# Four weight buffers and seven sets of activations at other places within a 512-byte line, in a two-block transformer kernel on one core

## The chip, the cores and the metric

The kernel runs on one core of one Trainium2 chip. Its time is the device time of one execution, in microseconds (us); with one core, that core is also the slowest. The profile is of one execution, and its span is the time from the first to the last of the program's own instructions.

## What is computed

Two blocks run one after the other on x of 256 tokens by 1024 columns, all in fp32. Cut to the matrix work, which is nearly all of the time:

```python
def first_block(...):
    h = rmsnorm(x, norm_mix_g[l])
    proj = h @ w_in[l]                      # 1024 x 8192: conv, stick-breaking, retention, gates
    up = jnp.einsum('bsnw,nwd->bsnd', branches, w_branch[l])
    x = x + jnp.sum(gates * up, axis=2) @ w_o[l]
    x = x + memory_attention(rmsnorm(x, norm_xa_g[l]), mem_n, w_xq[l], w_xkv[l], w_xo[l])
    x = x + squared_relu_mlp(rmsnorm(x, norm_mlp_g[l]), w_up[l], w_down[l])   # 1024 x 4096 and back
    return rmsnorm(x, final_g)

def second_block(...):
    # layer 0 mixes with ssd_mixer, layer 1 with mla_attention; after each mixer:
    h = layer_norm(DN_ALPHA * h + mix, ln_mix_g[i], ln_mix_b[i])
    ff = conv_ffn(h, ffn_up[i], ffn_conv_w[i], ffn_conv_b[i], ffn_down[i])    # 1024 x 5632, 2816 x 1024
    h = layer_norm(DN_ALPHA * h + ff, ln_ffn_g[i], ln_ffn_b[i])
```

## The kernel before

**Split products.** Every large product is taken three times in the type fp32r: each fp32 operand is split into a high part h and a rest l, and `mm3` adds h·h, h·l and l·h in PSUM. So each block of a weight matrix is needed as `wh` and `wl`, and each activation as `ah` and `al` (or another pair of that kind: `br`, `mt`, `memT`, `oT`, `gT`, `yT`, `cT`, each with an h and an l).

**Weights.** `chunk_plan` cuts all weights into some 200 chunks of at most 2048 columns of fp32 for each of the 128 partitions, and the host lays them out in the order of use. For each chunk `pump` issues one DMA from SyncE into `wr` (two buffers), `copy` makes `wh` from it on ScalarE, `sub` makes `wl` on VectorE. `wh` and `wl` have four buffers each, taken in turn by `ring`, so that the splits of later chunks run while TensorE works on an earlier one.

**Two kinds of products.** In `wstat` the weights are the stationary operand and the activations move: for each of eight blocks k of 128 rows, 256 columns of `ah` or `al` pass a 128x128 block of `wh` or `wl`. The rows of a profile write this as `mm<-ah,wh` (moving operand first). The order inside one k is (ah, wh), (al, wh), (ah, wl). In `xstat` the activations are stationary and up to 512 columns of the weights move: `mm<-wh,ah`, `mm<-wl,ah`, `mm<-wh,al`, and `mm<-wh,gTh` and so on in the down projections. Each matmul has a weight load (LDWEIGHTS, engine PEld) of its own, which runs beside the matmul before it.

**Order.** The program is recorded with an order of its own: `tick` decides from a table of estimated durations (class `Plan`) which waiting task or split is recorded next. Addresses do not enter into it. All recorded instructions stand at one line of the code (L284, the wrapper that records), so rows are told apart by their tiles.

**Places.** `new_act` gives each of seven layers its `ah` and `al`, from a pool with one buffer each, so all seven stand at one address. The `wh` and `wl` pools follow each other in SBUF, and a buffer is 8192 bytes long, a multiple of 512. Modulo 512, the built program has all four buffers of `wh` and all four of `wl` at 288, and `ah` and `al` at 480 in every layer. `br`, `gT`, `yT` and the `oT` of the first block are at 288, `mt`, `memT` and `cT` at 480. A row of `ah` for one k is 1024 bytes, a block of stationary columns 512 bytes, and all strides inside the buffers keep the place modulo 512, but for a few blocks of 320 and 384 columns in the attention's first product. `gap` puts an unused tile into a pool, to move what follows; only the attention of the second block does so.

Of the kernel before, what the change touches and what calls it, by code (L numbers as in the profile page):

```python
# [7 lines left out]
F32R = mybir.dt.float32r  # L8
# [8 lines left out]
P = 128  # L17
D = 1024
S = 256
ALPHA = 4 ** 0.25  # L20
NG = 8
RAW, HELD = 2, 4
# [64 lines left out]
def chunk_plan():  # L87
# [62 lines left out]
    def ffn(layer):  # L150
        for j in range(22):
            add("fu", K8, (f"fup{layer}", 128 * j, 128), (f"fup{layer}", 2816 + 128 * j, 128))
        xwide("fd", f"fdn{layer}", 22)

    ffn(0)
    for k in range(0, 8, 2):
        add("kvq", range(k, k + 2), ("kvd", 0, 320), ("qd", 0, 384))
# [305 lines left out]
        self.sync = Lane(plan, nc.sync, "sp")  # L463


class Kern:
    def __init__(self, nc, tc, a, dbg=None):
        self.at = Plan()
        self.nc, self.tc, self.a, self.dbg = Engines(nc, self.at), tc, a, dbg
        self.plan, _ = chunk_plan()  # L470
        self.nch = len(self.plan)
        self.n_dma = self.n_prep = self.n_half = self.n_get = self.n_done = 0
        self.raw, self.held, self.subs = {}, {}, []
        self.bg = []
        self.floor = 0.0
        self.turns = {}
        self.blocked, self.table = False, None
        self.work = self.skew = 0.0
        self.sums = np.concatenate([[0.0], np.cumsum([len(ks) * max(n, P) * UNIT for _, ks, _, n, _ in self.plan])])

# [12 lines left out]
            self.n_dma += 1  # L493

    def ring(self, pool, tag, dtype, n):
        t = pool.tile([P, 2048], dtype, tag=tag, name=tag)
        rows = self.turns.setdefault(tag, [])
        self.at.reuse(t, rows[-n] if len(rows) >= n else None)
        rows.append(t)
        return t  # L500
# [316 lines left out]

    def new_act(self):

        return (self.acts.tile([P, 8, S], F32R, tag="ah", name="ah"), self.acts.tile([P, 8, S], F32R, tag="al", name="al"), [0, 0])  # L820

    def ready(self, act, k, *taus):
        if len(act) == 3:
# [433 lines left out]
    def memory(self, x, mt, memT, mt_close):  # L1257
        nc, a = self.nc, self.a
        act = self.new_act()
        ga = self.bcast("xa", self.gb, "gb")  # L1260
        mp, mp_close = self.open("mem")
        oT = self.pair(mp, "oT", 8)

        kT = (mp.tile([P, 8, S], F32R, tag="kT", name="kT"), mt[1])
# [152 lines left out]
    def ssd(self, h, act):  # L1417
        nc, a = self.nc, self.a
        pool, close = self.open("ssd")
        yT = self.pair(pool, "yT", 16)  # L1420
        decs = Slots(self, pool, "dec", [P, 4, 384], F32, 4)
        r512 = Slots(self, pool, "r512", [P, 2, S], F32, 7)
        for i in range(2):
            t = self.gb.tile([P, D], F32, tag="gb", name="gb")
# [266 lines left out]
    def ffn(self, layer, h, act):  # L1691
        nc = self.nc
        pool, close = self.open(f"ffn{layer}")
        gT = self.pair(pool, "gT", 22)
        r512 = Slots(self, pool, "r512", [P, 2, S], F32, 6)

        def col(t):
            c = COLS["fcw"] + 132 * layer + t
            b = COLS["fcb"] + 44 * layer + t
            return lambda j: self.pcol[:, c + 44 * j:c + 44 * j + 1], self.pcol[:, b:b + 1]  # L1700

        def up_out(j):
            def run(pt, t):
                acc = yield from r512.wait()
                gs = [self.taps(acc[:, i, :], pt[:, 256 * i:256 * i + 256], 3, *col(j + 22 * i)) for i in range(2)]
                for g in gs:
                    next(g)
                yield "dve"
                for _ in zip(*gs):
                    pass  # L1710
                self.free(pt)
                yield "act"
                nc.scalar.activation(acc[:, 0, :], acc[:, 0, :], AF.Silu)
                yield "dve"
                nc.vector.tensor_mul(acc[:, 0, :], acc[:, 0, :], acc[:, 1, :])
                yield "act"
                yield from self.split((gT[0][:, j, :], gT[1][:, j, :]), acc[:, 0, :])
                r512.put(acc)
            return run

        tasks = []
        self.wmixed("fu", act, 8, [up_out(j) for j in range(MIXED["fu"][layer])], tasks)
        self.dump(("h1", "h2")[layer], h)
        for j in range(MIXED["fu"][layer], 22):
            self.wstat("fu", act, 8, up_out(j), tasks)
        g_, b_ = self.bcast(f"lfg{layer}", self.gb, "gb"), self.bcast(f"lfb{layer}", self.gb, "gb")
        act = None if layer else self.new_act()
        ps = self.xstat("fd", [2] * 11, self.lhs(gT), [(0, 512), (512, 1024)], tail=TAIL["fd"][layer],
                        before=lambda c: self.until(*tasks[2 * c:2 * c + 2]),
                        after=lambda t, p, got: self.layernorm(t, h, g_, b_, act, p, got))  # L1730
        close()
        return act
# [235 lines left out]
    def program(self):  # L1968
        nc, tc, a = self.nc, self.tc, self.a
        cs = []  # L1970

        def pool(name, bufs=1, **kw):
            cm = tc.tile_pool(name=name, bufs=bufs, **kw)
            cs.append(cm)
            return cm.__enter__()

        cp = pool("const")
        self.gb = pool("gb", 2)  # L1980
        self.dram = pool("dram", space=bass.MemoryType.DRAM)
        self.acts = pool("acts")
        cq = pool("small")
        self.tiny = pool("tiny", 4)
        self.tk = Slots(self, pool("tk"), "tk", [P, D], F32, 2)
        self.wraw, self.whi, self.wlo = pool("wraw", RAW), pool("whi", HELD), pool("wlo", HELD)
        pp = pool("ps", space=PSUM)
        self.mm = Slots(self, pp, "mm", [P, 512], F32, 4)
        self.sm = Slots(self, pp, "sm", [P, 512], F32, 4)

        x = cp.tile([P, 2, D], F32, tag="x", name="x")
        self.cst = cst = cq.tile([P, NCST], F32, tag="cst", name="cst")
        self.ones = cp.tile([P, P], F32, tag="ones", name="ones")
        nc.vector.memset(self.ones, 1.0)

        row = self.tk.get()
        o, w = ROWS["mix"]
        nc.sync.dma_start(out=row[0:1, :], in_=a["prow"][0:1, o:o + w])
        halves = [slice(512 * n, 512 * n + 512) for n in range(2)]
        for c in halves:  # L2000
            nc.sync.dma_start(out=x[:, 0, c], in_=a["x"][0:P, c])
        nc.sync.dma_start(out=cst[:, 0:P], in_=a["cst"][:, 0:P])
        self.pump(1)
        nc.sync.dma_start(out=x[:, 1, :], in_=a["x"][P:2 * P, :])
        self.pump()
        nc.sync.dma_start(out=cst[:, P:], in_=a["cst"][:, P:])
        gs = [self.mm.get() for c in halves]
        for pt, c in zip(gs, halves):
            self.mm1(pt, self.ones[0:1, :], row[0:1, c], True)
        self.tk.put(row)  # L2010
        self.pcol = cp.tile([P, NCOL], F32, tag="pcol", name="pcol")
        nc.sync.dma_start(out=self.pcol, in_=a["pcol"])
        self.ident, self.nu, self.ut = (cst[:, CST[n]:CST[n] + P] for n in ("ident", "nu", "ut"))
        self.at.one = cq.tile([1, 2], F32, tag="one", name="one")
        nc.vector.memset(self.at.one, 1.0)
        self.neg1 = cp.tile([P, P], F32, tag="neg1", name="neg1")
        nc.vector.memset(self.neg1, -1.0)
        self.mhalf = cq.tile([P, 2], F32, tag="mhalf", name="mhalf")
        nc.vector.memset(self.mhalf, -0.5)
        self.identb = cp.tile([P, P], BF16, tag="identb", name="identb")  # L2020
        nc.vector.tensor_copy(self.identb, self.ident)

        self.maskb = cp.tile([P, P], BF16, tag="maskb", name="maskb")
        nc.vector.memset(self.maskb, 0.0)
        nc.gpsimd.affine_select(out=self.maskb, in_=self.maskb, compare_op=ALU.is_ge, fill=-1e30, base=0,
                                pattern=[[-1, P]], channel_multiplier=1)

        act = self.new_act()
        self.until(self.spawn(self.rms(0, x, Halves(gs), act), first=True))

        def second():
            yield from self.rms(1, x, Halves(gs), act)
            for pt in gs:
                self.mm.put(pt)

        self.spawn(second(), first=True)
        mt, memT, mt_close = self.mixers(act)
        self.spawn(self.angles(cp))
        act, close = self.memory(x, mt, memT, mt_close)
        act = self.mlp(x, act, close)  # L2040
        act = self.ssd(x, act)
        act = self.ffn(0, x, act)
        act = self.attention(x, act)
        self.ffn(1, x, act)
        self.drain()
        assert self.n_get == self.nch
        for cm in reversed(cs):
            cm.__exit__(None, None, None)
# [21 lines left out]
```

## Time and profile before

| what | value |
|---|---|
| median of 2 runs | 1242.21 us (1240.86 to 1243.56) |
| the profiled execution | 1244.83 us |
| its span | 1243.1 us |
| busy PE, PEld, DVE, ACT, POOL | 1224.7, 1120.8, 853.9, 717.0, 53.5 us |
| matmuls and weight loads | 8468 each |
| read from HBM | 225.27 MB, 182 GB/s over the span |

A matmul's duration in the trace runs from its start to its modelled end and overlaps the next one's. How fast matmuls follow each other is read from starts, or from a stretch: in a stretch of length T that is filled with matmuls of one kind, each lasting d, a count of n means one start every (T + d) / n.

### The profile page before, as it was taken

How to read it: one execution, taken by the hardware profiler on the slowest of the kernel's cores; microseconds unless marked ns; L12 is line 12 of the kernel's file. 1: busy time of each engine (PE TensorE's matmuls, PEld its weight loads, DVE VectorE, ACT ScalarE, POOL GpSimd, SP SyncE). 2: the span in 40 equal slices, each digit the busy share in tenths (PEclk: the TensorE clock that was granted, in tenths of full speed). 3: DMA queues.
4: the chain of work that ended last, by engine and by line, in shares of the span. 5: the costliest groups of instructions: out<-in, count | busy, mean ns of one | idle time of the engine just before them, and what ended most of it. 6: DMA issues, size and time to landing. Idle time of an engine off the chain costs nothing.

```text
span 1243.1 us, 20768 instructions
## 1 busy us (share of the span) xinstructions
PE 1224.7 (99%) x8468; PEld 1120.8 (90%) x8468; DVE 853.9 (69%) x1378; ACT 717.0 (58%) x1181; POOL 53.5 (4%) x85
## 2 busy tenths in 40 slices
PE   7999999999999999999999999999999999999997
PEld 5978999989989998889999898999988888999986
DVE  5666847666746665446787797877765866888853
ACT  5666546446536554335788765666644575666641
POOL 0011000000000000000111201000000000000000
PEclk9999999999999999999999999999999999999999
DMA  7643355546544546524656555555573443455560
GB/s 254 235 167 127 146 196 219 179 156 228 176 152 159 214 172 221 201 106 166 227 190 233 193 174 194 187 172 202 184 259 118 161 181 123 172 197 182 213 256 35
DMA packets 35425, 227.71 MB, mean 183 GB/s; under 512 B 4321, under 2 KB 4993, under 8 KB 11522
## 3 DMA queue, kind: packets, MB, share of 16 engines
q1 hardware_dynamic: 35330, 226.39, 50.8%
q8 instruction: 66, 1.08, 0.4%
q14 instruction: 29, 0.24, 0.1%
HBM read 225.27 MB, written 1.10 MB: 182 GB/s over the span
## 4 chain that ended last, share of the span: by engine, by line
PE 95%; DVE 3%; DMA 1%; issue 0%; ACT 0%; POOL 0%; SPq 0%; POOLq 0%; DVEq 0%; ACTq 0%
PE mm L284 85%; PE sm L284 9%; DVE wl L284 1%; DVE x L284 1%; DMA wr<-wts 0%; DVE tk L284 0%; DMA cst<-cst 0%; POOL rs L284 0%; ACT wh L284 0%; DVE ln L284 0%; DVE al L284 0%; SPq L284 0%; POOLq L2066 0%; ACT r L284 0%; ACT ah L284 0%
## 5 line engine op out<-in xcount | busy, mean ns | idle before, releaser
L284 DVE TENSOR_TENSOR wl<-wr,wh 128x1024 fp32r<-128x1024 f32 (+3 forms) x408 | 479.4, 1198 | 173.7 <-ACT wh L284 173.0
L284 ACT CAST wh<-wr 128x1024 fp32r<-128x1024 f32 (+3 forms) x408 | 403.6, 1029 | 162.4 <-PE mm L284 87.9
L284 PE MATMUL mm<-ah,wh 128*128 128x256 f32 (+1 forms) x1496 | 421.1, 281 | 0.0
L284 PE MATMUL mm<-ah,wl 128*128 128x256 f32 (+1 forms) x1496 | 417.5, 279 | 0.0
L284 PE MATMUL mm<-al,wh 128*128 128x256 f32 (+1 forms) x1496 | 417.4, 279 | 0.0
L284 PEld LDWEIGHTS mm<-ah,wh 128*128 128x128 f32 (+1 forms) x1496 | 283.0, 189 | 1.6 <-issue 1.1
L284 PEld LDWEIGHTS mm<-ah,wl 128*128 128x128 f32 (+1 forms) x1496 | 281.0, 188 | 0.1
L284 PEld LDWEIGHTS mm<-al,wh 128*128 128x128 f32 (+1 forms) x1496 | 280.5, 188 | 0.4
L284 DVE SCALAR_TENSOR_TENSOR r<-mm,pcol,r 128x255 f32<-128x255 f32 (+2 forms) x212 | 86.9, 474 | 38.6 <-ACT r L284 38.6
L284 PE MATMUL mm<-wl,ah 128*128 128x512 f32 (+3 forms) x320 | 106.3, 338 | 3.1 <-DVE wl L284 3.0
L284 PE MATMUL mm<-wh,ah 128*128 128x512 f32 (+3 forms) x320 | 108.6, 345 | 0.0
L284 PE MATMUL mm<-wh,al 128*128 128x512 f32 (+3 forms) x320 | 105.9, 337 | 0.5 <-DVE al L284 0.5
L284 PE MATMUL mm<-wh,gTh 128*128 128x512 f32 x304 | 96.3, 391 | 0.0
L284 PE MATMUL mm<-wh,gTl 128*128 128x512 f32 x304 | 95.6, 389 | 0.0
L284 PE MATMUL mm<-wl,gTh 128*128 128x512 f32 x304 | 95.6, 390 | 0.0
L284 ACT ACTIVATE r<-mm,pcol 128x256 f32<-128x256 f32 x96 | 48.9, 560 | 46.9 <-PE mm L284 46.9
L284 PEld LDWEIGHTS mm<-wl,ah 128*128 128x128 f32 x320 | 60.3, 189 | 10.2 <-DVE wl L284 4.9
L284 PEld LDWEIGHTS mm<-wh,gTl 128*128 128x128 f32 x304 | 57.1, 188 | 11.8
L284 PEld LDWEIGHTS mm<-wl,gTh 128*128 128x128 f32 x304 | 57.1, 188 | 11.8
L284 PEld LDWEIGHTS mm<-wh,gTh 128*128 128x128 f32 x304 | 56.7, 188 | 12.0 <-issue 0.6
L284 PEld LDWEIGHTS mm<-wh,al 128*128 128x128 f32 x320 | 60.3, 189 | 7.0 <-DVE al L284 1.1
L284 PEld LDWEIGHTS mm<-wh,ah 128*128 128x128 f32 x320 | 60.3, 189 | 6.6 <-issue 0.7
(296 smaller groups left out, 1581.8 us busy)
## 6 DMA issues: line engine op xcount, KB each, us to landing
wr<-wts SPq DMA_DIRECT2D x186, 1024.0 KB, 4.9
wr<-wts SPq DMA_DIRECT2D x11, 768.0 KB, 4.3
gb<-prow SPq DMA_DIRECT2D x12, 512.0 KB, 6.8
dec<-rows SPq DMA_DIRECT2D x8, 768.0 KB, 7.5
wr<-wts SPq DMA_DIRECT2D x4, 704.0 KB, 4.2
wr<-wts SPq DMA_DIRECT2D x4, 512.0 KB, 7.0
tk<-mem SPq DMA_DIRECT2D x2, 512.0 KB, 7.9
out<-x SPq DMA_DIRECT2D x4, 256.0 KB, 2.1
```

What stands on the lines that cost most here:

```text
L284: r = f(*args, **kw)
```

## The change

Six edits, none of which adds, removes or reorders an instruction: on each of the five engines the instructions stand in the same order before and after, with the same tiles and shapes. One wait is added: of the second group of `dec` (the decay tiles of the state-space mixer), the first AFFINE_SELECT on GpSimd waits for ScalarE too, beside its DMA.

- The buffers of `wh` and `wl` become 16 elements (64 bytes) longer, so that the four of a ring stand 64 bytes apart modulo 512.
- `ah` and `al` get 128 elements more, and each layer takes its part from a start of its own, out of `PLACES` (bytes).
- Gaps stand ahead of `wl`, behind it, and at the start of the pools of the memory attention, the state-space mixer and the two feed-forward layers.
- The scratch for dynamic DMAs is 1 KB instead of 16 KB a partition; no DMA of this kernel uses it. It makes room for the rest.

```diff
+PLACE = 16
+PLACES = (0, 144, 256, 32, 288, 0, 16)
...
     def ring(self, pool, tag, dtype, n):
-        t = pool.tile([P, 2048], dtype, tag=tag, name=tag)
+        t = pool.tile([P, 2048 + (PLACE if dtype is F32R else 0)], dtype, tag=tag, name=tag)
...
     def new_act(self):
-        return (self.acts.tile([P, 8, S], F32R, tag="ah", name="ah"), self.acts.tile([P, 8, S], F32R, tag="al", name="al"), [0, 0])
+        at = PLACES[self.n_act] // 4
+        self.n_act += 1
+        h, l = (self.acts.tile([P, 8 * S + 128], F32R, tag=n, name=n)[:, at:at + 8 * S].rearrange("p (k s) -> p k s", s=S) for n in ("ah", "al"))
+        return (h, l, [0, 0])
...
         mp, mp_close = self.open("mem")
+        self.gap(mp, 288)
...
         pool, close = self.open("ssd")
+        self.gap(pool, 256)
...
         pool, close = self.open(f"ffn{layer}")
+        self.gap(pool, (32, 256)[layer])
...
-        self.wraw, self.whi, self.wlo = pool("wraw", RAW), pool("whi", HELD), pool("wlo", HELD)
+        self.wraw, self.whi = pool("wraw", RAW), pool("whi", HELD)
+        self.gap(pool("gap0"), 256)
+        self.wlo = pool("wlo", HELD)
+        self.gap(pool("gap1"), 256)
...
-    nc = bacc.Bacc("TRN2", target_bir_lowering=False, num_devices=1)
+    nc = bacc.Bacc("TRN2", target_bir_lowering=False, num_devices=1, dynamic_dma_scratch_size=1024)
```

Places modulo 512 in the two built programs:

| tiles | before | after |
|---|---|---|
| `wh`, `wl`, the four buffers in the order of use | 288, 288, 288, 288 | 288, 480, 416, 352 |
| `wr` (both buffers) | 288 | 288 |
| `ah`, `al`: mixers, memory attention, MLP | 480, 480, 480 | 480, 112, 224 |
| `ah`, `al`: state-space mixer, feed-forward 0 | 480, 480 | 0, 256 |
| `ah`, `al`: latent attention, feed-forward 1 | 480, 480 | 480, 496 |
| `br`; `memT`, `mt`; `cT` | 288; 480; 480 | 288; 480; 480 |
| `oT`, `kT`, `qs`, `vt` of the memory attention | 288 | 64 |
| `gT` of MLP, feed-forward 0, feed-forward 1 | 288, 288, 288 | 288, 320, 32 |
| `yT` | 288 | 32 |

## Rows read from the trace of the kernel before

**Rows 1.** The page: span, then busy time (share) and instructions by engine.

```profile
span 1243.1 us, 20768 instructions
PE 1224.7 (99%) x8468; PEld 1120.8 (90%) x8468; DVE 853.9 (69%) x1378; ACT 717.0 (58%) x1181; POOL 53.5 (4%) x85
...
PEclk9999999999999999999999999999999999999999
```

**Rows 2.** The page, chain that ended last: shares of the span by engine, by line.

```profile
PE 95%; DVE 3%; DMA 1%; issue 0%; ACT 0%; POOL 0%; SPq 0%; POOLq 0%; DVEq 0%; ACTq 0%
```

**Rows 3.** Waits of PE: for whom, us in total, times, longest.

```profile
PE sm L284 <- DVE tk L284: 3.1, 1, 3.1
PE mm L284 <- DVE wl L284: 3.0, 3, 2.0
PE mm L284 <- DMA tk<-prow: 2.4, 1, 2.4
```

**Rows 4.** Stretches: busy us (x instructions) of PE, PEld, DVE, ACT, POOL; clock; DMA share, GB/s.

```profile
139.00:180.00 41.00, 41.00 (x364) 41.00 (x363) 23.24 (x29) 21.53 (x33) 0.00 (x0) 1.00 0.54 193
240.00:252.00 12.00, 12.00 (x102) 12.00 (x101) 11.62 (x22) 5.94 (x9) 0.00 (x0) 1.00 0.68 254
...
402.00:468.00 66.00, 66.00 (x562) 66.00 (x562) 44.06 (x50) 37.58 (x50) 0.00 (x0) 1.00 0.55 200
484.00:540.00 56.00, 56.00 (x249) 46.40 (x248) 24.55 (x21) 20.07 (x20) 0.00 (x0) 1.00 0.52 188
...
798.00:898.00 100.00, 100.00 (x851) 100.00 (x850) 82.19 (x145) 63.22 (x109) 0.00 (x0) 1.00 0.52 179
1083.00:1172.00 89.00, 89.00 (x788) 89.00 (x787) 75.25 (x134) 58.44 (x99) 0.00 (x0) 1.00 0.56 194
```

**Rows 5.** PE's groups by form, feed-forward 0, 798 to 898 us.

```profile
L284 PE MATMUL mm<-ah,wl 128*128 128x256 f32 x284 | 79.9, 281 | 0.0
```

**Rows 6.** The same for feed-forward 1, 1083 to 1172 us.

```profile
L284 PE MATMUL mm<-ah,wl 128*128 128x256 f32 x262 | 72.4, 276 | 0.0
```

**Rows 7.** PE's groups by form over the span: busy us, mean ns of one | idle before.

```profile
L284 PE MATMUL mm<-ah,wh 128*128 128x256 f32 x1488 | 418.9, 281 | 0.0
L284 PE MATMUL mm<-ah,wl 128*128 128x256 f32 x1488 | 415.3, 279 | 0.0
L284 PE MATMUL mm<-al,wh 128*128 128x256 f32 x1488 | 415.2, 279 | 0.0
...
L284 PE MATMUL mm<-wh,gTl 128*128 128x512 f32 x304 | 95.6, 389 | 0.0
...
L284 PE MATMUL mm<-wh,al 128*128 128x512 f32 x144 | 57.3, 398 | 0.5 <-DVE al L284 0.5
...
L284 PE MATMUL mm<-wl,ah 128*128 128x256 f32 x144 | 40.4, 281 | 0.3 <-DVE wl L284 0.3
...
L284 PE MATMUL mm<-brh,wl 128*128 128x256 f32 x96 | 27.2, 283 | 0.0
...
L284 PE MATMUL mm<-memTh,wl 128*128 128x256 f32 x64 | 17.7, 276 | 0.0
```

**Rows 8.** All operations on tile brh: ns min/median/max, first and last start us.

```profile
L284 PEld LDWEIGHTS mm<-brh,wl x96: 187/192/193, 182.6 to 251.6; 128*128 128x128 f32 x96
L284 PE MATMUL mm<-brh,wl x96: 279/283/284, 182.7 to 251.7; 128*128 128x256 f32 x96
```

**Rows 9.** The page, groups of DVE and ACT that make wl and wh.

```profile
L284 DVE TENSOR_TENSOR wl<-wr,wh 128x1024 fp32r<-128x1024 f32 (+3 forms) x408 | 479.4, 1198 | 173.7 <-ACT wh L284 173.0
L284 ACT CAST wh<-wr 128x1024 fp32r<-128x1024 f32 (+3 forms) x408 | 403.6, 1029 | 162.4 <-PE mm L284 87.9
```

**Rows 10.** GpSimd in order of time: start us, us, the second group of dec among them.

```profile
631.01 1.23 POOL L284 TENSOR_SCALAR_AFFINE_SELECT dec<-dec 128x512 f32<-128x512 f32 x2
633.48 3.51 POOL L284 TENSOR_SCALAR_AFFINE_SELECT dec<-dec 128x512 f32<-128x512 f32 x2 [1.24 <-DMA dec<-rows]
```

More of the change, by code (lines that the diff above doesn't have):

```diff
@@ L477, in __init__ @@
         self.blocked, self.table = False, None
+        self.n_act = 0
         self.work = self.skew = 0.0
```

## The prediction

> **What bounds the kernel now.** I read the page first: PE is busy for 1224.7 of 1243.1 us, the clock is granted in full in all 40 slices [rows 1], and 95% of the chain that ended last is PE's [rows 2]. The longest wait of PE in the whole run is 3.1 us [rows 3]. So nothing that makes PE wait is worth a per cent, and the time can only move if matmuls follow each other at another rate. Busy time can't show that, because a matmul's row overlaps the next one's. The count of starts in a filled stretch can.
>
> Four stretches hold nothing but matmuls of 256 moving columns (up to a few small ones at their edges). By (T + d) / n, feed-forward 0 starts one every (100 + 0.281) us / 851 = 117.8 ns, the MLP's up projection one every (66 + 0.281) / 562 = 117.9 ns, feed-forward 1 one every (89 + 0.276) / 788 = 113.3 ns, and the gates one every (41 + 0.276) / 364 = 113.4 ns [rows 4]. The first and the third run the same code with the same shapes from the same places, at the same full clock, with DVE at 82% and 85% and ACT at 63% and 66%. PE's own row tells the two rates apart: a matmul lasts 281 ns at the slower [rows 5] and 276 ns at the faster [rows 6]. The reader is to see a stream with two stable rates, which keeps one of them through a whole stage of twenty chunks.
>
> A third rate is in the branch product, where the moving `br` and all `wh` and `wl` stand at 288: one start every (12 + 0.283) / 102 = 120.4 ns, and 283 ns a matmul [rows 4, 7]. There the weight load takes 192 ns in the median, with 187 ns as the shortest [rows 8]: what is slow is the pair, the load and the matmul beside it. With `memT` at 480 against 288, the distance that `ah` has, a matmul lasts 276 ns [rows 7]. So distance 0 (modulo 512) was slow in all its chunks, and distance 192 is either.
>
> What the neighbours do is not the cause, as far as rows show: DVE and ACT are as busy at the fast rate as at the slow one [rows 4].
>
> With 512 moving columns the load has twice the time. The MLP's down projection, `gT` at 288 against 288, starts one every (56 + 0.389) / 249 = 226.5 ns [rows 4], twice the fast rate, and 389 ns a matmul [rows 7]. With `ah` at 480 as the stationary side, one lasts 398 ns [rows 7]; part of that is waits at the start of a layer.
>
> **What the best rate would return.** Durations of 276, 281 and 283 ns go with 113.3, 117.8 and 120.4 ns from start to start, so 5 ns of duration are about 4.5 ns of time.
> - `ah`, `al` moving, 3 x 1488 matmuls at 279 ns (281 in the first group, which also holds the waits at the start of a chunk): 3 of 5 ns above the fast rate, so 60% of them are slow. 4464 x 0.6 x 4.5 ns = 12.1 us [rows 7].
> - `br`: 3 x 96 x (120.4 - 113.3) ns = 2.0 us [rows 7].
> - Weights moving with 256 columns, 3 x 144 at 281 ns: all slow, 432 x 4.5 ns = 1.9 us [rows 7].
> - Weights moving with 512 columns against `ah`, 3 x 144 at 398 against 389 ns: 9 x 0.9 x 432 = 3.5 us at the most, since waits are in it; I take 2 [rows 7].
> - The other products of 512 columns are at the fast rate: nothing.
>
> Together 18 us, 1.4% of the span. No row of 256 columns goes under 276 ns in its mean, so I have no ground for a rate below 113.3 ns.
>
> **The change part by part.**
>
> *Four places for the weight buffers, seven for the activations.* The distance of moving to stationary side was 192 in every chunk of `ah`. Now it is another one in each of four chunks in turn: 192, 0, 64, 128 in the mixers and the latent attention, for instance, and four others in each other layer. For none but 0 and 192 does a row of 256 moving columns in `wstat` show a rate. The ends: all at 113.3 ns gives the 18 us back. All at 120.4 ns costs 4464 x (0.4 x 7.1 + 0.6 x 2.6) ns = 19.6 us, and 9 x 0.9 x 912 ns = 7.4 us if the 512 columns of `gT` took on the 398 ns: +27 us. Between ends so far apart I go by the row that is nearest to a chunk of its own: today a stage stays at one rate for all its chunks because each meets the last one's distance again. With the distance changed at each chunk, a slow rate is no longer handed on to the next by equal places. I take half of the slow excess of `ah` as gone: 6 us of the 12, and 2 of the 3.9 with weights moving.
>
> *Branch product.* One chunk in four keeps distance 0. The other three get 320, 384 and 448. At the middle rate for these the gain is 216 x 2.6 ns = 0.6 us, at the best one 216 x 7.1 ns = 1.5 us. I take 1.
>
> *The gaps* move `gT`, `yT`, `oT`, `kT` and `vt`. With 512 moving columns, distance 0 runs at the best rate already, so there is little to gain; about 0.5 us lies in the small products. I take 0, with the 7.4 us above as the price if it goes wrong.
>
> *Making the splits.* The casts of 1029 ns and the subtractions of 1198 ns [rows 9] write to other places. Should each become 5% longer, 408 x 60 ns = 24 us more on DVE would bring it from 69% to 71% of the span; PE's stream hides that, since its waits for `wl` are 3.0 us in all [rows 3]. If they became shorter, it would return no more than those 3.0 us. I take 0.
>
> *The added wait* on GpSimd stands ahead of the select at 631 us (1.23 us for two), which feeds decay tiles [rows 10]. Behind it in GpSimd's queue are the next two selects, which started at 633.5 us after a wait of 1.24 us for their own DMA. An early ACT instruction costs nothing; a late one would first use up that 1.24 us, and past it delays the decays of one of four groups, beside chunks of products that PE has in hand. I take 0, and 3 us (the length of the later selects) as its upper end.
>
> *The scratch* is not read or written by any instruction: 0.
>
> Sum: -6 - 2 - 1 = -9 us. Against the profiled execution, 1244.8 us (its span of 1243.1 and 1.7 around it), that is 1235.8 us. This execution lies 2.6 us above the median of the two runs shown, and the three times differ by 4.0 us, about what one stage like feed-forward 0 costs by its choice of rate (851 x 4.5 ns = 3.8 us). I hold the sum against the median, 1242.2: 1233 us.
>
> [...] The rows show one and the same kind of matmul at 276, 281 and 283 ns, at full clock [rows 5 to 7]. [...]
>
> **The rivals.**
> - *The place does not set the rate.* Something else at the start of a stage picks one of the two rates, and it picks as before, or by another throw. For it: feed-forward 0 and 1 differ at the same places [rows 4]. Against it: `br` is slow in all its chunks [rows 8]. The time is 1242 us, give or take the 4 us of one stage's throw.
> - *Every stream at the best rate.* The places are such that load and moving stream do not meet in any layer. For it: 113.3 ns is stable over twenty chunks once reached. Against it: the mixers and the latent attention now have distance 0, the slow one, in a quarter of their chunks. The time is 1242 - 18 = 1224 us.
> - *More meetings than before.* With four distances in each layer, most of them near each other, a load that meets the moving stream costs the 120.4 ns of `br` in most chunks. At three chunks of four the mean is 118.6 ns against 113.3 + 0.6 x 4.5 = 116.0 now: 4464 x 2.6 ns = +11.6 us, 1254 us. It turns from gain to loss when more than 2.7 / 7.1 = 38% of the chunks are at 120.4 and the rest at 113.3. For it: distance 0, which the kernel before had in `br` alone, now comes in the mixers too. Against it: only 0 is seen to be always slow.
>
> **How the numbers follow.** A measurement of this kernel can tell about 2% from no change. The forecast of 1233 us gets 0.45, no effect of the place 0.17, all at the best rate 0.20, more meetings 0.18. The best rate everywhere is 1.4% below the median, so faster by over 2% (below 1217 us) needs a rate that no row shows: 0.02. Slower by over 2% (above 1267 us) needs nearly all of the +27 us: 0.03. The range from 1222 to 1250 us holds the forecast, the best rate and no effect, and part of the losing case. The forecast's own range is 1227 to 1239.
>
> **What would show each step right or wrong.** In the profile after, the group of 256 columns with `ah` over the span should have a mean of 277 to 278 ns in place of 279, `br` 279 to 281 in place of 283, and the stretches of the MLP's up projection and of feed-forward 0 should hold chunks at both 113 and 118 ns, with changes at the borders of chunks. The matmuls of 512 columns with `gT` should stay at 389 ns, PE's waits below 10 us in all. If whole stages still keep one rate, or if feed-forward 1 falls back to 118 ns, the step on the chunks is wrong. A mean of 281 ns or more would make it slower than before.

## The result and the profile after

The changed kernel takes 1259.53 us (median of 1259.25 and 1259.81) against 1242.21: 1.0139 times as long, with an interval of 1.0091 to 1.0188. The profiled execution after is the one of 1259.25 us, with a span of 1257.5; the one before had a span of 1243.1 [rows 1], so 14.4 us are to be found.

The page of the changed kernel: span, busy time by engine, the chain's shares, and the groups that make `wl` and `wh`.

```profile
span 1257.5 us, 20769 instructions
PE 1240.6 (99%) x8468; PEld 1129.6 (90%) x8468; DVE 854.5 (68%) x1378; ACT 716.4 (57%) x1181; POOL 53.4 (4%) x85
...
PE 95%; DVE 2%; DMA 1%; issue 0%; SPq 0%; ACT 0%; POOL 0%; POOLq 0%; DVEq 0%
...
L284 DVE TENSOR_TENSOR wl<-wr,wh 128x1024 fp32r<-128x1024 f32 (+3 forms) x408 | 480.0, 1199 | 178.2 <-ACT wh L284 177.3
L284 ACT CAST wh<-wr 128x1024 fp32r<-128x1024 f32 (+3 forms) x408 | 403.0, 1028 | 163.2 <-PE mm L284 94.6
```

Only PE has changed: 15.9 us more busy time with the same 8468 matmuls, while DVE, ACT and GpSimd stand where they stood [rows 1], and cast and subtraction take what they took [rows 9]. PE's waits have not grown either [rows 3]; these are the changed kernel's (for whom, us in total, times, longest):

```profile
PE mm L284 <- DVE wl L284: 2.7, 3, 1.6
PE mm L284 <- DMA tk<-prow: 2.4, 1, 2.4
PE sm L284 <- DVE tk L284: 2.3, 1, 2.3
```

So the time lies in the rate. The stretches of the changed kernel that answer to [rows 4], with the same columns:

```profile
139.00:180.00 41.00, 41.00 (x354) 41.00 (x353) 22.33 (x28) 20.52 (x33) 0.00 (x0) 1.00 0.53 189
402.00:468.00 66.00, 66.00 (x569) 66.00 (x567) 45.11 (x51) 37.02 (x49) 0.00 (x0) 1.00 0.53 192
484.00:540.00 56.00, 56.00 (x244) 45.56 (x244) 23.61 (x20) 20.15 (x21) 0.00 (x0) 1.00 0.53 190
798.00:898.00 100.00, 100.00 (x850) 100.00 (x849) 81.32 (x146) 63.55 (x111) 0.00 (x0) 1.00 0.52 187
1083.00:1172.00 89.00, 89.00 (x761) 89.00 (x760) 73.86 (x134) 57.91 (x100) 0.00 (x0) 1.00 0.51 178
```

By (T + d) / n, with the durations shown below, the gates went from one start every 113.4 ns to 116.6, the MLP's up projection from 117.9 to 116.5, feed-forward 0 from 117.8 to 118.0, feed-forward 1 from 113.3 to 117.3, and the down projection with `gT` from 226.5 to 231.1. The clock is 1.00 in all of them. What was slow gained little or nothing; what was fast lost.

PE's groups by form over the span, changed kernel, beside [rows 7]:

```profile
L284 PE MATMUL mm<-ah,wh 128*128 128x256 f32 x1488 | 420.5, 283 | 0.0
L284 PE MATMUL mm<-ah,wl 128*128 128x256 f32 x1488 | 417.0, 280 | 0.0
L284 PE MATMUL mm<-al,wh 128*128 128x256 f32 x1488 | 416.7, 280 | 0.0
...
L284 PE MATMUL mm<-wh,gTl 128*128 128x512 f32 x304 | 97.0, 394 | 0.0
...
L284 PE MATMUL mm<-wh,al 128*128 128x512 f32 x144 | 57.4, 399 | 0.5 <-DVE al L284 0.5
L284 PE MATMUL mm<-wl,ah 128*128 128x256 f32 x144 | 40.6, 282 | 0.3 <-DVE wl L284 0.3
...
L284 PE MATMUL mm<-brh,wl 128*128 128x256 f32 x96 | 26.8, 279 | 0.0
```

`ah` and `al` moving are 1 to 2 ns a matmul slower, not 1 to 2 ns faster; `gT` is 5 ns slower; `br` is 4 ns faster. To see what that is in time I added up, over each whole trace, the time from each matmul's start to the next one's, by what the matmul multiplies:

| products (matmuls) | before, us | after, us | difference |
|---|---|---|---|
| `ah`, `al` moving, 256 columns (4488) | 523.8 | 532.6 | +8.8 |
| `gT` and weights, 512 columns (912) | 207.9 | 211.9 | +4.0 |
| weights moving past `ah`, 512 and 256 columns (864) | 159.0 | 160.1 | +1.1 |
| `memT`, `oT`, `yT`, `cT`, `mt` (930) | 181.1 | 183.6 | +2.5 |
| `br` (288) | 34.7 | 33.8 | -0.9 |
| fp32 products and the rest | 126.3 | 125.3 | -1.0 |

Together +14.5 us, against the 14.4 between the two spans.

Then chunk by chunk. The MLP's up projection in the changed kernel, four chunks in a row, PE's groups by form; the moving place stands 256, 320, 384 and 448 bytes (modulo 512) above that of the weights:

```profile
L284 PE MATMUL mm<-ah,wl 128*128 128x256 f32 x15 | 4.2, 283 | 0.0
...
L284 PE MATMUL mm<-ah,wl 128*128 128x256 f32 x15 | 4.1, 276 | 0.0
...
L284 PE MATMUL mm<-ah,wl 128*128 128x256 f32 x15 | 4.2, 281 | 0.0
...
L284 PE MATMUL mm<-ah,wl 128*128 128x256 f32 x15 | 4.1, 276 | 0.0
```

283, 276, 281, 276 ns go with 120.0, 113.4, 118.5 and 113.6 ns from start to start, and this rotation comes back in every group of four. Once it is under way, feed-forward 0 has 118.3, 116.8, 119.8 and 117.4 ns in rotation, at distances 480, 288, 352 and 416; feed-forward 1 has 116.6 to 118.3 at 16, 80, 144 and 208, where it had 113.3 throughout.

### The profile page after: what moved, and what is told of

Its sections match the earlier page's. It is cut to its first block, busy times and chain, and to the rows that moved or that the text cites. A ratio compares the mean times of both kernels' runs of the same rounds, so it can differ in the third digit from the quotient of the medians.

```text
span 1257.5 us, 20769 instructions
## 1 busy us (share of the span) xinstructions
PE 1240.6 (99%) x8468; PEld 1129.6 (90%) x8468; DVE 854.5 (68%) x1378; ACT 716.4 (57%) x1181; POOL 53.4 (4%) x85
## 4 chain that ended last, share of the span: by engine, by line
PE 95%; DVE 2%; DMA 1%; issue 0%; SPq 0%; ACT 0%; POOL 0%; POOLq 0%; DVEq 0%
PE mm L284 86%; PE sm L284 9%; DMA wr<-wts 1%; DVE wl L284 1%; DVE x L284 0%; SPq L284 0%; DVE tk L284 0%; DVE al L284 0%; POOL rs L284 0%; DVE ln L284 0%; ACT wh L284 0%; POOLq L2080 0%; ACT r L284 0%; DVEq L2080 0%; ACT ah L284 0%
```

## The experiments

The theory that this suggests: the distance of the moving place from the stationary one, modulo 256, sets the rate of a chunk by itself, and the chunk before it has no say. Rivals: that the changing of distances from chunk to chunk costs time, whichever they are; that a wait, a gap or the smaller scratch does it; and, from the prediction, that the place does not matter at all.

Edits are against the kernel before. Every kernel has the 1 KB scratch of the first, and in each all places that are not named are those of before. "Filled stretch" is PE alone from 806 to 890 us, inside feed-forward 0: busy us (x matmuls), clock, DMA share, GB/s; the spacing is (84 + d) / n with d of 0.276 to 0.283 us. Each kernel ran beside the kernel before on the same chip; the second time given is that kernel's. The ratio and its 95% interval are worked out from all runs, so the ratio is not always the quotient of the two medians. In all kernels `ring` and `new_act` are those of the change, with `PLACE` and all `PLACES` at 0 unless the edit says otherwise; so `ah` and `al` are 512 bytes longer everywhere, which keeps all places modulo 512.

### The scratch alone

```diff
-    nc = bacc.Bacc("TRN2", target_bir_lowering=False, num_devices=1)
+    nc = bacc.Bacc("TRN2", target_bir_lowering=False, num_devices=1, dynamic_dma_scratch_size=1024)
```

> Control: of the change only the scratch of 1 KB, all operands at their places modulo 512 of before. Theory A (the distance moving minus stationary, modulo 256, sets the rate of a matmul): the time of before, 1242 us, mean of the 256-column group of ah 279 ns, gT at 389 ns. Rival (the scratch or the absolute address costs): up to 17 us more, gT above 392 ns.

1240.28 us against 1240.23: 1.0003 [0.9988, 1.0019]. The scratch costs nothing. The profile taught something else; its filled stretch:

```profile
806.00:890.00 84.00, 84.00 (x744) 1.00 0.53 189
```

84.276 / 744 = 113.3 ns, where the profiled execution of before had feed-forward 0 at 117.8 [rows 4]. No place differs, so at distance 192 a stage has either of two rates. This profile's span is 1237.1 us, 6.0 under that of [rows 1], and 4.8 us of it are in the products of `ah`: feed-forward 0 and the first four chunks of moving `ah` (27 to 49 us) ran at 117.8 ns in the profile that I predicted from, at 113.3 here. The times speak for a difference between executions of one and the same program: of ten runs of this kernel on one chip six lie between 1238.8 and 1240.3 us and four between 1242.9 and 1244.5, some 4 us apart, as one such stage would have it. The changed kernel's two lie 0.6 us apart.

### The weight buffers alone

```diff
+PLACE = 16
...
+        self.gap(pool("gap0"), 256)
+        self.wlo = pool("wlo", HELD)
+        self.gap(pool("gap1"), 256)
```

> Only the four weight buffers staggered by 64 bytes (288, 480, 416, 352), all activations and pools at the places of before. Theory A, with the rates by distance read from the trace after the change: ah +5.6 us (distances 192, 0, 64, 128 at 115.6, 119.7, 115, 118.6 ns against 116.0 now), gT +3.0 us (distances 0, 192, 128, 64 at 227, 233, 232, 229 ns), br -1.1, yT and oT +0.8: about +8 us, 1250. Rival B (any stagger costs, because the distance changes at each chunk border): the same sign here, parted from A by the 128-byte stagger. Rival C (only the odd places of the activations, off the 32-byte grid of before, cost): 1242 here.

1255.22 against 1240.23: 1.0122 [1.0103, 1.0142]. With `ah` at 480 in every layer the chunks go through distances 192, 0, 64, 128, and each keeps its own rate, now in feed-forward 0 too: 120.0 ns at 0, 113.4 at 64, 118.5 at 128, 113.6 at 192. PE's groups over the chunk at distance 0 and the one at 64:

```profile
L284 PE MATMUL mm<-ah,wl 128*128 128x256 f32 x15 | 4.2, 283 | 0.0
...
L284 PE MATMUL mm<-ah,wl 128*128 128x256 f32 x15 | 4.1, 276 | 0.0
```

By start to start, `ah` lost 5.5 us against the profile of before and 10.3 against that of the scratch alone, and `gT`, which itself was not moved, 3.4. Its group over the span went from 389 ns [rows 7] to 393:

```profile
L284 PE MATMUL mm<-wh,gTl 128*128 128x512 f32 x304 | 96.7, 393 | 0.0
```

The expected +8 us were reckoned from the one profile of before with its slow stages, and so were too few.

### The activations alone

```diff
+PLACES = (0, 144, 256, 32, 288, 0, 16)
```

> Only the seven places of the activations, weights all at 288, pools as before. Theory A: distances 192, 336, 448, 224, 480, 192, 208; feed-forward 1 goes from 113.3 to 117.2 ns (+3.5 us), the memory attention's queries to 120 (+1.2), the state-space mixer +1.6, the MLP's up projection from 117.7 to 114.7 (-1.9), feed-forward 0 +0.5: +5 us, 1247, gT stays at 389 ns. Rival B: 1242 or less, no stagger. Rival C: nearly the whole +17 us, 1259.

1252.37 against 1240.23: 1.0098 [1.0082, 1.0114]. Here every chunk of a layer has the same distance, so nothing changes from chunk to chunk, and it is slower all the same. Feed-forward 0, at distance 480, starts one matmul every 118.3 ns in all its chunks, feed-forward 1, at 208, one every 119.2. The filled stretch:

```profile
806.00:890.00 84.00, 84.00 (x713) 1.00 0.53 187
```

So time is lost without any alternation, and more than the +5 us expected: feed-forward 1 came at 119.2 ns in place of 117.2, and the MLP, at 448, stayed at 117.8 in place of 114.7. The two halves are no sum: +15 us for the weights, +12 for the activations, +17 for both. Where the weights already rotate, another start of `ah` only sends the chunks to four other distances.

### Weights 128 bytes apart

```diff
+PLACE = 32
```

> Weight buffers staggered by 128 bytes in place of 64 (288, 160, 32, 416), activations and pools as before: the distances of ah are 192, 320, 448, 64, all of the kind that ran at 113.4 to 115.8 ns after the change. Theory A: ah -5 to -11 us, gT +3 us (distances 0, 384, 256, 128), yT and oT +0.8: 1233 to 1241, with the chunks of ah at 113.4 ns mostly. Rival B (stagger as such costs): as the 64-byte stagger, 1250 or more.

1242.32 against 1240.23: 1.0012 [0.9996, 1.0029], a little over the expected range. The chunks go through 192, 320, 448 and 64, without 0 and 128. In the MLP and both feed-forward layers the first one to four half chunks come at 117.7 ns, and all later ones at 113.3; the filled stretch shows it:

```profile
806.00:890.00 84.00, 84.00 (x743) 1.00 0.54 192
```

In this profile `ah` gained 6.7 us against that of before (the throw of the scratch alone gave 4.8), and `gT` gave 3.0 us back, at 392 ns. The net is no difference that the measurement shows. The distance changes at each chunk here as it does with 64 bytes, and the 15 us of that stagger do not appear: the rival that the alternation as such costs time falls.

### Distance 0 in every chunk

```diff
+PLACES = (320, 320, 320, 320, 320, 320, 320)
```

> All weights at 288 as before, and the activations of all seven layers at 288 too: distance 0 in every chunk of ah. Theory A (distance sets the rate): 120 ns in every such chunk, 4488 x 5.4 ns = +24 us against the control, -1 us where 512 columns of the weights move past ah: 1263 us, ah at 283 ns in the mean. Rival (the place only biases which of two rates a stage falls into, as I predicted): stages at 113 and 118 ns remain, at most +15 us, 1255.

1263.49 against 1243.04: 1.0178 [1.0155, 1.0201]. One number, the start of `ah` within its tile, makes the kernel 20 us slower. In every layer the chunks run at 120.0 ns; the filled stretch and the group over the span:

```profile
806.00:890.00 84.00, 84.00 (x703) 1.00 0.49 176
```

```profile
L284 PE MATMUL mm<-ah,wl 128*128 128x256 f32 x1488 | 421.0, 283 | 0.0
```

That the place does not matter is out. Nor is it the place of `ah` as such: distance 0 gave 120.0 ns with both operands at 288 here, and with both at 480 in the run of the weight buffers alone.

One chunk of the state-space mixer is an exception that tells something. Its stationary blocks have 32 columns in place of 128 and lie 128 bytes apart (one more exception to the strides of the other buffers), so that `ah` is at distance 0 and 128 in turn. Rows of this run, from 565 to 590 us:

```profile
L284 PE MATMUL mm<-al,wh 128*32 128x256 f32 x8 | 2.2, 276 | 0.0
L284 PEld LDWEIGHTS mm<-al,wh 128*32 128x32 f32 x8 | 0.9, 108 | 0.2
```

From the fifth of its 24 matmuls on they start every 113.3 ns, and the ones with 128 columns right behind every 120.0. The matmul moves the same 256 columns; what is shorter is the weight load, 108 ns against the 187 to 193 of a block with 128 columns [rows 8]. In this one chunk, and likewise in the run at distance 128 (276 and 277 ns a matmul), the slow rate went with the full load.

### The pools' gaps alone

```diff
+        self.gap(mp, 288)
...
+        self.gap(pool, 256)
...
+            self.gap(pool, (32, 256)[layer])
```

> Only the gaps at the start of the pools: gT of feed-forward 0 at 320 and of feed-forward 1 at 32, yT at 32, the memory attention's tiles at 64; weights 288, activations 480. Theory A: 512 columns past gT at distance 480 cost 264 x 6 ns = 1.6 us, at distance 256 nothing much, yT 0.5, oT 0.6: about +3 us, 1243. Rival (the gaps carry what the weights' and the activations' places don't add up to): more than +6 us or less than 0.

1239.12 against 1243.04: 0.9987 [0.9969, 1.0004]. `gT` lost 1.4 us: in feed-forward 0, at distance 480, its matmuls follow each other by 233.3 ns once under way, in feed-forward 1, at 256, by 226.7, as at 0. `oT` lost 0.5 us. The rest is again a throw of `ah` (-7.9 us in this profile). So by its time alone the rival (less than 0) could stand; the products show that it is the throw and not the gaps.

### Distances 192 and 448 in turn, and br off the weights' place

```diff
+PLACE = 64
...
+        self.gap(mp, 192)
```

> Weight buffers staggered by 256 bytes (288, 32, 288, 32), activations at 480, br moved to 480. Theory A with a period of 256 bytes: distances 192 and 448 are one, ah as in the control or better if the alternation shakes a stage out of the slow rate; gT at 0 and 256 stays at 389 ns; br goes from 120 to 113.4 ns, -1.9 us: 1234 to 1239. Rival (period 512): gT at distance 256 costs 450 x 3 to 6 ns = +1.4 to +2.7 us, and half the chunks of ah get a rate of their own: 1242 or more.

1238.52 against 1243.04: 0.9979 [0.9962, 0.9996]. 192 and 448 both ran at 113.3 ns in this profile's filled stretch, and both at 117.8 in its MLP; `br`, now at 480, lasts 276 ns in place of 283 [rows 7], 1.8 us in all. The gap stands here at the start of the mixers' pool, ahead of `br`.

```profile
806.00:890.00 84.00, 84.00 (x744) 1.00 0.56 195
```

```profile
L284 PE MATMUL mm<-brh,wl 128*128 128x256 f32 x96 | 26.5, 276 | 0.0
```

### Only wl at distance 0

```diff
+        self.gap(pool("gap0"), 192)
+        self.wlo = pool("wlo", HELD)
+        self.gap(pool("gap1"), 320)
```

> wl alone moved to 480, the place of ah; wh at 288, all else as before. Theory A1 (what counts is the distance between the moving operand and the weight load that runs beside it, the one for the next matmul): only the start after (al, wh), beside which wl is loaded, is slow: 120 ns there, 113 to 115 ns after the two others, +9 us for ah, and +1.8 us for gT after (wl, gTh) at distance 192: about 1250. Theory A2 (the matmul's own stationary block counts): the slow start is the one after (ah, wl). Rival (neither): all three alike.

1261.72 against 1243.04: 1.0162 [1.0139, 1.0184], some 12 us over the 1250 expected. `wl` stands at 480, the place of `ah`, and `wh` stays at 288. I had wanted to see whether the load of the slow buffer or the matmul beside it pays. In the filled stretch neither answer came: the starts behind (ah, wh), (al, wh) and (ah, wl) follow by 118.3, 117.5 and 117.5 ns, as they do in the slow stage of the kernel before, and PE's groups are all alike:

```profile
L284 PE MATMUL mm<-ah,wh 128*128 128x256 f32 x239 | 67.2, 281 | 0.0
L284 PE MATMUL mm<-ah,wl 128*128 128x256 f32 x239 | 67.2, 281 | 0.0
L284 PE MATMUL mm<-al,wh 128*128 128x256 f32 x238 | 66.9, 281 | 0.0
```

The gates and feed-forward 1, which ran at 113.3 ns in every profile with all weights at distance 192, are at 117.8 here too: with one of three products at distance 0, all three kept the slower of the two rates.

In one stretch the answer did come. PE's groups from 28 to 48 us, the first four chunks of moving `ah`:

```profile
L284 PE MATMUL mm<-al,wh 128*128 128x256 f32 x56 | 16.2, 290 | 0.0
L284 PE MATMUL mm<-ah,wl 128*128 128x256 f32 x55 | 15.5, 283 | 0.0
L284 PE MATMUL mm<-ah,wh 128*128 128x256 f32 x55 | 15.5, 283 | 0.0
```

There the starts behind (al, wh), beside which `wl` is loaded, come after 127.7 ns, those behind (ah, wh) and (ah, wl) after 121.7 and 117.3. The slow one is that of theory A1, so the slow start went there with the load beside the matmul, and not with the matmul's own block. Why this shows in these four chunks alone stays open.

### Activations of three layers at 96, weights alternating

```diff
+PLACE = 64
+PLACES = (0, 0, 128, 0, 128, 0, 128)
...
+        self.gap(mp, 192)
```

> Put together from what the runs so far showed: weight buffers staggered by 256 bytes, br at 480 (distance 192 or 448), and the activations of the MLP and of both feed-forward layers at 96, so that their chunks of ah have distance 320 and 64, and the products of 256 moving weight columns in the same layers 192 and 448 in place of 320 and 64. Theory A: these 432 matmuls, at 117.8 ns in every run so far, go to 113.4 to 115 ns, -1 to -1.9 us; br -1.8 us as in the run with 256 bytes; ah stays at 114.3 ns in the mean: 1234 to 1238 against 1238.5 to 1243 for before. Rival (320 and 64 are not as good as 192 and 448 for ah, the slow rate is kept there): ah +5 us or more, 1243 or more.

1245.44 against 1239.83: 1.0042 [1.0029, 1.0056], a miss. With distances of 64 and 320 alone, MLP and both feed-forward layers stayed at 117.8 ns to the last chunk, once the first 24 matmuls were past:

```profile
806.00:890.00 84.00, 84.00 (x715) 1.00 0.53 189
```

So 64 and 320 are of the kind with two rates (113.4 ns at 64 with the weight buffers alone, at 320 in the changed kernel's MLP), and being able to run at 113.3 ns does not mean that a stage will. The 432 products with 256 weight columns moving gained 0.8 us against the profile of before, under the 1 to 1.9 expected.

### Distance 128 in every chunk

```diff
+PLACES = (448, 448, 448, 448, 448, 448, 448)
```

> All weights at 288, all activations at 416: distance 128 in every chunk of ah. Theory A: 118.5 ns in each, 4488 x 3.9 ns = +17.5 us against the control, and +1 us for 512 columns of weights past ah at distance 384: about 1258. Rival (118.5 ns came from the alternation with chunks at other distances, not from 128 itself): 113 or 118 by stage, 1238 to 1250.

1258.68 against 1239.83: 1.0151 [1.0137, 1.0164], with 118.5 to 118.8 ns in all chunks of the filled stretches but the first four of moving `ah` (26 to 49 us), which ran at 120.0. So 128 has a slow rate of its own, without a 0 among the chunks; why those four were slower still stays open.

```profile
806.00:890.00 84.00, 84.00 (x710) 1.00 0.50 176
```

### br alone, and the alternation once more

```diff
+        self.gap(mp, 192)
```

> Only br moved from 288 to 480 (a gap of 192 bytes ahead of it); all weights at 288, all activations at 480. Theory A: br at 113.4 ns in place of 120, -1.8 us, the rest as before with its throw of some stages: ratio 0.9985, 1238 to 1242. Rival (br's gain in the run with 256 bytes came from the alternation of the buffers): br stays at 117.8 ns or more, at most -0.7 us.

> The run with 256 bytes once more, beside the one with br alone, for its time: buffers at 288 and 32 in turn, br at 480. Theory A with a period of 256: the same as br alone, ratio 0.9985. Rival (alternation keeps more stages at the fast rate): 2 to 4 us below br alone, ratio 0.996.

The first has this one line, the gap ahead of `br`, the second is the kernel of 192 and 448 in turn again. `br` alone: 1240.37 against 1241.93, 0.9983 [0.9967, 0.9999], with `br` at 276 ns. With the alternation as well: 1241.44, 0.9997 [0.9981, 1.0012], and this time its feed-forward 0 ran at the slower rate:

```profile
806.00:890.00 84.00, 84.00 (x715) 1.00 0.54 189
```

The same program has thus run its feed-forward 0 at either rate. The two profiles are from different chips, but the two groups of times of the scratch-only kernel, on one chip, speak against the chip as the cause. The -0.2% of the first run was thus in part a lucky throw; alternating by 256 does not choose the rate. The best version I found is `br` moved alone: 1.8 us in its profile, 0.17% in the times, at the edge of what an interval shows.

## Why the prediction was wrong

I forecast 9 us less, and the kernel takes 17 us more.

**What bounds the kernel.** Right: PE's rate is all there was to move. Every experiment's difference is one of start-to-start spacing, and no PE wait grew by more than 1.2 us.

**The ceiling of 18 us.** Not contradicted: no run had matmuls of 256 columns below 113.3 ns. But part of the 12 that I put down to `ah` was this one execution's throw, not a loss that stood in every execution: the profiles of the scratch, of the gaps, of `br` alone and of 192 and 448 in turn (two) spent 1.3 to 7.9 us less on `ah`.

**The step that failed** is the one on the chunks: "With the distance changed at each chunk, a slow rate is no longer handed on to the next by equal places. I take half of the slow excess of `ah` as gone: 6 us of the 12, and 2 of the 3.9 with weights moving." Measured: `ah` +8.8 us against the profile of before, and +13.6 against the scratch-only kernel (519.0 us by start to start); weights moving +1.1. The sign that I had named came: feed-forward 1 fell back from 113.3 to 117.3 ns. The step took the unknown distances to be no worse than 192, and most of them are slow. The runs put this in its place, for 256 columns in filled stretches (distance is moving minus stationary place):

| distance modulo 256 | start to start, ns | where |
|---|---|---|
| 0 | 120.0 | `br` before (120.4 by count), all chunks of one run, some in two others |
| 128 | 118.5 to 118.7 | one run (but for its first four chunks), some chunks in two others |
| 64, 192 | 113.3 to 113.6, or 117.8 | all chunks of before and of seven experiments, some in three other runs |
| others (16, 32, 80, 96, 144, 160, 208, 224) | 116.6 to 119.8 | the changed kernel, activations alone |

In these runs the place set what a chunk could run at, and in the kernel before every chunk of `ah` already stood at one of the only two distances measured with the best rate, 113.3 ns. The change leaves two of four chunks there in the mixers and the MLP, whose starts of `ah` are multiples of 64 away from the weights', and none in the memory attention, the state-space mixer and the two feed-forward layers, whose starts are not. (The latent attention, which I counted with the mixers, has no product in which `ah` moves past the weights: there weights of 320 and 384 columns move past `ah`, and their time did not change.) Handing on was half right: the MLP's chunks at 320 and 448 ran at 113.4 and 113.6 ns between slow ones, and with 64 and 192 in turn a slow start gave way to 113.3 in three layers. But chunks at the other distances were slow by themselves, at 116.6 to 120.0 ns, and nothing was won by passing from one to another.

The row was there to see. `br` at 120.4 ns in all its chunks [rows 4, 8] said that a distance can be slow by itself; I had it as the price of distance 0 and then took the nearest row for the unknown distances from a stage at 192.

**The second miss** is a term that I set under the wrong edit. I priced `gT` at 7.4 us under the pools' gaps and took 0. The gaps alone cost 1.4 us of `gT`; the staggered weights alone cost 3.4, since they take three of four buffers off distance 0, where 512 columns ran best (227 ns from start to start in the MLP of the changed kernel, against 229 to 233 at the other three). The profile after, feed-forward 0 with `gT`, from 910 to 960 us:

```profile
L284 PE MATMUL mm<-wl,gTh 128*128 128x512 f32 x72 | 23.0, 395 | 0.0
```

395 ns here and 394 over the span, against the 389 that I said should stay. With the other wide products (`oT`, `yT`, `mt`, weights past `ah`) it is some 6 us of the 14.4.

**`br`, -1 us.** Right: -0.9 measured. All operations on `brh` in the changed kernel, ns as least, median, most:

```profile
L284 PEld LDWEIGHTS mm<-brh,wl x96: 187/188/192, 183.9 to 252.7; 128*128 128x128 f32 x96
...
L284 PE MATMUL mm<-brh,wl x96: 274/280/285, 184.1 to 252.8; 128*128 128x256 f32 x96
```

The weight load's median fell from 192 to 188 ns with the matmul's from 283 to 280 [rows 8], as the quarter of chunks left at distance 0 would have it.

**The splits, the wait, the scratch, 0 each.** Right. GpSimd in order of time after:

```profile
635.81 1.23 POOL L284 TENSOR_SCALAR_AFFINE_SELECT dec<-dec 128x512 f32<-128x512 f32 x2
638.41 3.26 POOL L284 TENSOR_SCALAR_AFFINE_SELECT dec<-dec 128x512 f32<-128x512 f32 x2 [1.37 <-DMA dec<-rows]
```

The select with the added wait shows none in its row, and the next still waits for its own DMA, 1.37 us against 1.24 [rows 10].

**The rivals.** "More meetings than before" is nearest to what happened, but only half by its mechanism: distance 0 came in a quarter of the chunks of the mixers and the MLP, while most of the loss came at distances that it had no rate for. Its 1254 us were short, because it knew one slow rate where there are several, and no price for `gT`. That the place sets nothing fell with the run at distance 0 (1.0178): in the filled stretch the same matmuls with the same loads took 120.0 ns there and 113.3 in the run of the scratch alone, with one operand at another place. What the rival of the unset place said of a throw at the start of a stage was true of distances 64 and 192: both were needed. **The range** ended at 1250 because I gave the losing case 18% and cut it in the middle.

What stays open: what picks 113.3 or 117.8 ns at distances 64 and 192. DVE and ACT are as busy at either [rows 4]. It is no even throw: in the six profiles with `ah` at 192 (or 448) in all chunks, the gates' stretch of [rows 4] and feed-forward 1 ran at 113.3 ns each time, feed-forward 0 three times, the MLP once. 64 mixed with 192 ran at 113.3 ns in the one profile of it, and nine of that kernel's ten times lie within 1.6 us, where the scratch-only kernel spreads over 5.7; that fits a choice by mixing the two, but I have not shown it.

## What to carry to other kernels

Where PE never waits, count starts in a filled stretch, chunk by chunk, against the place of both operands modulo 256 bytes (the period that these runs showed); a loop that keeps one distance may already stand on the best one, and here spreading the places out averaged over the bad ones and cost 17 us. Narrow and wide moving sides ran best at different distances here (256 columns at 64 or 192, 113.3 ns at best; 512 columns at 0, 226.7 ns), so a move of shared weight buffers must be priced for every product that reads them. And profile the kernel before more than once: a stage's rate that differs between executions is not a loss to count on winning back.

## What the runs showed of the hardware that was not expected

- For 256 fp32r columns the rate went with the distance modulo 256, not 512: 0 and 256 both 120.0 ns, 128 and 384 both 118.5.
- For 512 columns distance 0 (or 256) was the best: 226.7 to 228 ns where all chunks had it; 64 and 320 gave about 229, all other distances seen 232 to 235.
- At 64 and 192 there were two stable rates, 113.3 and 117.8 ns, which differed between executions of the same program; the kernel before spread over 4.5 to 9.9 us in 9 to 23 runs and three other kernels with `ah` at 192 in all chunks over 4.7 to 5.8 us in ten to twelve, those with all chunks at 0 or 128 over 2.1 and 0.5 us in only four.
- A distance off the multiples of 64 is not fully told by the distance: 208 ran at 116.7 ns between other distances in the changed kernel, and at 119.2 where all chunks had it. The weights stood at 32 modulo 64 in every run, so for these the runs don't part the distance from the place of the moving operand itself.
- One product of three at distance 0 held all three at 117.5 to 118.3 ns in the filled stretch, and in the first four chunks slowed most the start behind the matmul beside which its weights were loaded (127.7 ns).
- With a weight load of 32 columns (108 ns) distance 0 and 128 cost nothing: 113.3 ns in the one chunk that has it, in two runs.
